# Retention's up projection in seven-product units, after the pooling branch's

## The chip, the cores and the metric

The kernel runs on one core of a Trainium2 chip. The metric is the device time of one execution in microseconds (us). The kernel before has a median of 1364.72 us over 3 runs (1364.48 to 1365.15).

## The reference: one decoder block with two token mixers

Input x is 1024 tokens by 1024 features in float32. One layer computes

```
h  = rmsnorm(x);  z = h @ w_in          # q | k | v | g | pool channels | gate logits
ret_n = group_norm(retention(q, k, v))  # 4 heads, chunks of 128 tokens
y_ret  = (silu(g) * ret_n * gn_gain) @ w_ret_up            # 1024 -> 1024
p[g]   = mean over the last 2/4/8/16 tokens of pool channels - the token itself
y_pool = (group_linear(p) * pool_scale) @ w_pool_up        # 512 -> 1024
gates  = sigmoid(gate_logits + b_gate)                     # 2 x 1024
x  = x + (gates_A * y_ret + gates_B * y_pool) @ w_o
x  = x + relu(rmsnorm(x) @ w_up)^2 @ w_down                # 4096 wide
out = rmsnorm(x)
```

## The kernel before

Activations are kept feature-major: 8 tiles (f = 0 to 7) of 128 features by 1024 tokens, in two halves of 512 tokens. Every float32 operand of a matmul is a *pair*: its rounding to fp32r (an ACTIVATE Copy on ScalarE) and the remainder (a subtraction on VectorE); `split_pair` (L133) makes one for 128x512. A product of two pairs takes three matmul passes, `PASSES` (L114).

A plain projection (`feature_major`, L126) multiplies 8 k-tiles by 3 passes for each output tile and half: 24 matmuls of 128x512. The other form is the *unit*: `Unit` (L180) and `seven` (L212) treat weight and activation as 2 x 2 blocks and form the four output blocks of two feature tiles, over both token halves, from seven block products (B11, T2, B21, T1, T3, B22, T4) instead of eight. A block product is 4 k-tiles by 3 passes, 12 matmuls; a unit has 84. For this a unit makes four sums of weight blocks (L202) and seven weight pairs, one `pair_tile` of tag "a" each (L203), and seven sets of four activation pairs (`hx` or `h2`) must exist. The results meet in PSUM banks X, Y, Z and V: p1 is a copy of X, u2 = p1 - Y, u4 = u2 + Z, and `done(m, half, ps, add)` takes each finished block on. With `late=True` (the first unit of a row) k = 3 comes after k = 0 to 2 of all four banks.

The order of the work:

1. q, k, v and retention per head (L480 to L494). `transposed` (L468) writes the normalized result to retn_dram.
2. `pool_input` (L502) makes the pooling channels and stores them in u_dram; `mixed_blocks` (L512) makes the activation sums T1 to T4 as `hx`.
3. Twelve mixer units (`mixer_unit`, L541). Units 0 to 3 are swish units: they make g, its swish from a Sigmoid and a product (L566 to L570), multiply it with ret_n and store the result in ret_dram. Units 4 to 11 are gate units: Sigmoid (L573), stored in sg_dram, tiles 0 to 7 for retention (A) and 8 to 15 for pooling (B). In unit 11, `load_ret` (L584) reads ret_dram back as 16 pairs retT.
4. Retention's up projection as a plain one (L630 to L641, ps_yr): 8 tiles, each multiplied by its gate from sg_dram (L638). After every second tile comes one group of pooling (`pool`, L604): VectorE's window sums and `exact` products with pool_w (ps_pw), giving ypT.
5. Pooling's up projection (L643 to L660, ps_yp), its gate, the sum with retention's part, and the pairs mixT.
6. The output projection (L698 to L723, ps_o), plain, which also makes x1, its squares and `h2`.
7. Sixteen up units (`up`, L732) and the down projection (L860 on).

Three things set the order. The kernel is written in program order, and the Tile framework's scheduler places each instruction on its engine's queue when, by its own timing, operands and buffers are there, earlier instructions first; on the chip each queue then runs in that fixed order. Buffers come from pools by tag: "h" and "r" have 16 tiles each and "a" 9 (L68), 4 KB per partition each; `wpool` has 4 weight tiles, `rpool` 2 "raw" tiles; PSUM has 5 "mm" and 3 "aux" banks. An instruction that needs a tile waits until an old one of its tag is let go. And loads go through SyncE's queue (SP), stores and some loads through GpSimd's (POOL).

Of the kernel before, what the change touches and what calls it, by code (L numbers as in the profile page):

```python
# [10 lines left out]
F32 = mybir.dt.float32  # L11
# [5 lines left out]
P = 128  # L17
# [5 lines left out]
NH = 4  # L23
# [15 lines left out]
def block_kernel(ctx: ExitStack, tc: tile.TileContext, a: dict, out: bass.AP):  # L39
# [12 lines left out]
    idle = apool.tile([P, HALF], mybir.dt.bfloat16, tag="a", name="idle", bufs=9)  # L52
# [13 lines left out]
    mask = consts.tile([P, NH, CH], F32, name="mask")  # L66
    corr = consts.tile([P, 4, 16], F32, name="corr")
    BUFS = {"h": 16, "r": 16, "a": 9}  # L68
# [47 lines left out]
    def product(ps, nk, stationary, moving):  # L116
        n = nk * len(PASSES)
        i = 0
        for k in range(nk):
            for sa, sb in PASSES:  # L120
                nc.tensor.matmul(  # L121
                    ps, stationary(k, sa), moving(k, sb), start=i == 0, stop=i == n - 1
                )
                i += 1

    def feature_major(ps, w, x, half, nk=KT, j0=0):  # L126
        product(
            ps, nk,
            lambda k, s: w[:, s, k, j0 : j0 + P],
            lambda k, s: x[k][half][:, s, :],  # L130
        )
# [48 lines left out]
    class Unit:  # L180


        def __init__(self, name, src):
            self.name, self.ws = name, {}
# [12 lines left out]

        def stationary(self, x):
            if x not in self.ws:
                src, *adds = self.made[x]  # L200
                for dst, u, v in adds:
                    nc.vector.tensor_tensor(dst, u, v, ALU.add)  # L202
                self.ws[x] = pair_tile("a", f"w{x}_{self.name}")  # L203
                split_pair(self.ws[x], src)
            return self.ws[x]
# [80 lines left out]
    R1 = a_tile("a", "R1")  # L286
# [181 lines left out]
    def transposed(h, rn):  # L468
        for e in range(2):
            dst = a_tile("a", f"retn{h}_{e}")  # L470
# [31 lines left out]
    def pool_input(g):  # L502
        w = load_piece(a["w_fm"][8 + g], f"w_pu{g}")
        u = a_tile("a", f"u{g}")
        for half in range(2):
            sl = slice(half * HALF, (half + 1) * HALF)
            ps = mm_bank(f"ps_pu{g}_{half}")
            feature_major(ps, w, hT, half)
            nc.scalar.activation(u[:, sl], ps, AF.Copy)
        nc.gpsimd.dma_start(u_dram[g], u)  # L510
# [27 lines left out]
    ret_dram = dram_tile("ret_dram", (KT // 2, P, 2, S))  # L538
    sg_dram = dram_tile("sg_dram", (2 * KT, P, S))

    def mixer_unit(i, first=None, after=None):  # L541
# [9 lines left out]
        def done(m, half, ps, add=None):  # L551
# [3 lines left out]
            if swish:  # L555
                t = rpool.tile([P, 2, HALF], F32, tag="raw", name=f"sw{f}_{half}")
                z, sig = t[:, 0, :], t[:, 1, :]
            else:
                z = ps if add is None else dst
# [4 lines left out]
            if swish:  # L564
                nc.vector.scalar_tensor_tensor(z, y, sign, R1[:, sl], ALU.mult, ALU.mult)
                nc.scalar.activation(sig, z, AF.Sigmoid)  # L566
                nc.vector.scalar_tensor_tensor(
                    dst, dst, vec[:, V_GNG + f : V_GNG + f + 1], sig, ALU.mult, ALU.mult
                )
                nc.vector.tensor_tensor(dst, dst, z, ALU.mult)  # L570
            else:
                nc.vector.tensor_tensor(z, y, R1[:, sl], ALU.mult)
                nc.scalar.activation(  # L573
                    dst, z, AF.Sigmoid, scale=sign, bias=vec[:, V_BG + f : V_BG + f + 1]
                )
            left[m] -= 1
            if not left[m]:
                nc.gpsimd.dma_start(ret_dram[f // 2, :, f % 2, :] if swish else sg_dram[f], o[m])
# [3 lines left out]
    retT = []  # L582

    def load_ret():  # L584
        for p2 in range(KT // 2):
            r2 = w_tile(f"ret{p2}", F32).rearrange("p (i t) -> p i t", i=2)
            nc.sync.dma_start(r2, ret_dram[p2])
            for i in range(2):
                retT.append([])
                for half in range(2):  # L590
                    dst = pair_tile("h" if p2 < 2 else "r", f"retT{2 * p2 + i}_{half}")
                    split_pair(dst, r2[:, i, half * HALF : (half + 1) * HALF])
                    retT[-1].append(dst)

    for i in range(12):
        mixer_unit(i, first_mx if i == 0 else None, load_ret if i == 11 else None)


    pw_raw, pw = a_tile("r", "pw_raw", shape=(P, HALF)), pair_tile("r", "pw")
    nc.sync.dma_start(pw_raw, a["pool_w"])  # L600
    split_pair(pw, pw_raw)
    ypT = []

    def pool(g):  # L604
        win = WINDOWS[g]
        u = a_tile("r", f"uf{g}")
        nc.sync.dma_start(u, u_dram[g])
        nc.vector.tensor_tensor(u, u, R1, ALU.mult)
        cur = u
        step = 1  # L610
        while step < win:
            nx = a_tile("r", f"s{g}_{step}")
# [6 lines left out]
        ypT.append([])  # L619
        for half in range(2):  # L620
            pooled = pair_tile("r", f"pooled{g}_{half}")
            split_pair(pooled, cur[:, half * HALF : (half + 1) * HALF])
            ps = aux_bank(f"ps_pw{g}_{half}")
            exact(ps, lambda s: pw[:, s, g * P : (g + 1) * P], lambda s: pooled[:, s, :])
            dst = pair_tile("h", f"ypT{g}_{half}")
            split_scaled(dst, ps, vec[:, V_PSC + g : V_PSC + g + 1])
            ypT[g].append(dst)

    mixed = []
    for f in range(KT):  # L630
        w = load_piece(a["w_ret"][f], f"w_ret{f}")
        m = a_tile("a", f"m{f}")
        nc.sync.dma_start(m, sg_dram[f])
        for half in range(2):
            sl = slice(half * HALF, (half + 1) * HALF)
            ps = mm_bank(f"ps_yr{f}_{half}")
            feature_major(ps, w, retT, half)
            nc.vector.tensor_tensor(m[:, sl], m[:, sl], ps, ALU.mult)  # L638
        mixed.append(m)
        if f % 2:  # L640
            pool(f // 2)  # L641
    mixT = []
    for f in range(KT):  # L643
        if f % 2 == 0:
            w = load_piece(a["w_pool"][f // 2], f"w_po{f}", cols=256)
            sg = w_tile(f"sgb{f}", F32).rearrange("p (i t) -> p i t", i=2)
            nc.sync.dma_start(sg, sg_dram[KT + f : KT + f + 2].rearrange("i p t -> p i t"))
        m = mixed[f]
        pairs = []
        for half in range(2):  # L650
# [3 lines left out]
            y = sg[:, f % 2, sl]  # L654
            nc.vector.tensor_tensor(y, y, ps, ALU.mult)
            nc.vector.tensor_tensor(m[:, sl], m[:, sl], y, ALU.add)
            dst = pair_tile("h", f"mixT{f}_{half}")
            split_pair(dst, m[:, sl])
            pairs.append(dst)
        mixT.append(pairs)  # L660
# [36 lines left out]

    for k in range(4):  # L698
# [4 lines left out]
        ws = {}  # L703
        for n, (f, half) in enumerate(order):
            if k == 3 and n == 1:
                first_up = Unit("up0", a["w_up"][0]).begin(B11, T2, T1, T3)
            if f not in ws:
                x1[f] = a_tile("a", f"x1_{f}")
                nc.gpsimd.dma_start(x1[f], a["xT"][f * P : (f + 1) * P, :])
                ws[f] = load_piece(a["w_o"][f], f"w_o{f}")  # L710
                gained[f] = a_tile("r", f"gained{f}")
            sl = slice(half * HALF, (half + 1) * HALF)
            ps = mm_bank(f"ps_o{f}_{half}")
            feature_major(ps, ws[f], mixT, half)
# [8 lines left out]
        moving_operands(h2, k, gained[k], gained[k + 4], "r" if k < 2 else "h")  # L723
# [8 lines left out]
    def up(j):  # L732
# [8 lines left out]
        def done(m, half, ps, add=None):  # L741
# [16 lines left out]
            Unit(f"up{j}", a["w_up"][j]) if j else first_up, h2, done, late=j == 0,  # L758
# [137 lines left out]
    u4s = [a_tile("a", f"u4_{i}", shape=(P, 2, HALF)) for i in range(2)]  # L896
# [195 lines left out]
```

## Time and profile before

| | before |
|---|---|
| median of 3 runs | 1364.72 us |
| the profiled execution | 1365.59 us, its span 1363.5 us |
| mixer units, from unit 0's second pass to the end of unit 11 | 297.9 to 512.6 us |
| ps_yr with ps_pw | 512.6 to 605.9 us |
| ps_yp | 605.9 to 649.4 us |
| ps_o | 649.4 to 740 us, some up products among it |
| VectorE busy in ps_yp's stretch | 32.79 of 43.5 us |

The profile is one execution on the chip. PE is TensorE, PEld its weight loads, DVE VectorE, ACT ScalarE, POOL GpSimd, SP SyncE. L12 is line 12 of the kernel. A group of instructions is shown as `out<-in`, partitions x elements, count, busy time, mean ns of one, and the idle time of the engine before it with what ended it. The chain is the work that ended last, followed back from the end; its rows give start, length and what ran. A wait's row gives the total, the number of times and the longest. A DMA's row ends with the size and the median time from issue to landing.

### The profile page before, as it was taken

To read this page: it belongs to the slowest core of one execution; us is meant where nothing else is said; L and a number is where in the kernel's file an instruction comes from. 1 tells how busy PE (TensorE), PEld (TensorE's weight loads), DVE (VectorE), ACT (ScalarE), POOL (GpSimd) and SP (SyncE) were. 2 spreads that over 40 slices of the span, in tenths; PEclk is the share of its full clock that TensorE was granted. 3 is DMA by queue.
4 is the path that set the end of the run, shared out by engine and by line. 5 is a ranking of instruction groups with operands and counts; after the bars stand their busy time and mean duration, and the time that the engine had idled before them with its cause. 6 is when DMAs were issued, how large, how long until landed. Compare 5 with 4: busy or idle time off the path is not lost.

```text
span 1363.5 us, 17493 instructions
## 1 busy us (share of the span) xinstructions
PE 1350.9 (99%) x6572; PEld 1137.6 (83%) x6572; DVE 988.8 (73%) x1627; ACT 569.0 (42%) x968; POOL 85.6 (6%) x151
## 2 busy tenths in 40 slices
PE   9999999999999999999999999999999999999997
PEld 6998989888888888888888888888888888888886
DVE  5765565689966668728667888877787967689675
ACT  6224425564334343113445443343433544444372
POOL 0000001111000000000000011110111000000000
PEclk9999999999999999999999999999999999999999
DMA  9112021364352266224422244433438989778423
GB/s 361 50 63 77 17 93 63 100 240 170 108 185 90 97 249 236 77 78 170 139 93 81 112 170 170 170 127 128 170 140 311 410 315 360 257 267 310 152 71 124
DMA packets 65444, 225.07 MB, mean 165 GB/s; under 512 B 7376, under 2 KB 9424, under 8 KB 61264
## 3 DMA queue, kind: packets, MB, share of 16 engines
q1 hardware_dynamic: 47152, 158.66, 32.9%
q0 software_dynamic: 17920, 65.02, 12.6%
q8 instruction: 51, 0.84, 0.2%
q10 hardware_dynamic: 288, 0.29, 0.1%
q14 instruction: 33, 0.27, 0.1%
HBM read 167.31 MB, written 56.62 MB: 164 GB/s over the span
## 4 chain that ended last, share of the span: by engine, by line
PE 93%; DMA 2%; issue 2%; ACT 1%; DVE 1%; POOL 0%; SPq 0%; POOLq 0%; DVEq 0%; ACTq 0%
PE ps_v L121 7%; PE ps_o L121 6%; PE ps_yr L121 6%; PE ps_dnZ L864 6%; PE ps_Xup L219 6%; PE ps_dnX L864 6%; PE ps_Zup L219 6%; PE ps_dnV L864 6%; PE ps_Vup L219 6%; PE ps_Xmx L219 5%; PE ps_Zmx L219 4%; PE ps_Vmx L219 4%; PE ps_kT L121 3%; PE ps_yp L121 3%; PE ps_pu L121 3%; PE ps_qT L121 3%
## 5 line engine op out<-in xcount | busy, mean ns | idle before, releaser
L121 PE MATMUL ps_v<-w_v_hi,hT 128*128 128x256 f32 x512 | 96.0, 284 | 0.0
L134 ACT ACTIVATE w_up<-raw_up 128x512 fp32r<-128x512 f32 x96 | 58.5, 627 | 89.6 <-DVE raw_up L202 45.4
L219 PE MATMUL ps_Xup<-mv,w_up 128*128 128x512 f32 x384 | 93.2, 390 | 0.0
L864 PE MATMUL ps_dnX<-db,da 128*128 128x512 f32 x384 | 93.0, 389 | 0.1
L219 PE MATMUL ps_Zup<-mv,w_up 128*128 128x512 f32 x384 | 92.8, 389 | 0.0
L219 PE MATMUL ps_Vup<-mv,w_up 128*128 128x512 f32 x384 | 92.4, 389 | 0.0
L121 PE MATMUL ps_yr<-retT,w_ret 128*128 128x512 f32 x384 | 88.3, 389 | 0.5 <-ACT w_ret L94 0.5
L121 PE MATMUL ps_o<-mixT,w_o 128*128 128x512 f32 x384 | 87.7, 389 | 0.0
L121 PEld LDWEIGHTS ps_yr<-retT,w_ret 128*128 128x128 f32 x384 | 72.0, 188 | 15.8 <-ACT w_ret L94 0.9
L864 PEld LDWEIGHTS ps_dnX<-db,da 128*128 128x128 f32 x384 | 72.0, 188 | 15.4 <-DVE db L135 0.5
L219 PEld LDWEIGHTS ps_Vup<-mv,w_up 128*128 128x128 f32 x384 | 72.1, 188 | 15.0
L219 PEld LDWEIGHTS ps_Zup<-mv,w_up 128*128 128x128 f32 x384 | 72.1, 188 | 14.9
L121 PEld LDWEIGHTS ps_o<-mixT,w_o 128*128 128x128 f32 x384 | 72.0, 188 | 15.0
L219 PEld LDWEIGHTS ps_Xup<-mv,w_up 128*128 128x128 f32 x384 | 71.9, 188 | 14.9
L135 DVE TENSOR_TENSOR w_up<-raw_up,w_up 128x512 fp32r<-128x512 f32 x96 | 64.6, 687 | 26.2 <-ACT w_up L134 26.1
L121 PEld LDWEIGHTS ps_v<-w_v_hi,hT 128*128 128x128 f32 x512 | 80.7, 192 | 0.0
L134 ACT ACTIVATE w_mx<-raw_mx 128x512 fp32r<-128x512 f32 x72 | 43.7, 628 | 81.4 <-DVE raw_mx L202 39.7
L121 PE MATMUL ps_v<-w_v_lo,hT 128*128 128x256 f32 x256 | 72.6, 284 | 0.0
L219 PE MATMUL ps_Xmx<-hT,w_mx 128*128 128x512 f32 x288 | 69.8, 389 | 0.0
L219 PE MATMUL ps_Vmx<-hx,w_mx 128*128 128x512 f32 x288 | 69.5, 389 | 0.0
L739 ACT ACTIVATE act<-act 128x512 f32<-128x512 f32 x64 | 40.2, 629 | 62.7 <-DVE act L738 60.6
L219 PEld LDWEIGHTS ps_Vmx<-hx,w_mx 128*128 128x128 f32 x288 | 54.1, 188 | 11.2
(250 smaller groups left out, 2826.3 us busy)
## 6 DMA issues: line engine op xcount, KB each, us to landing
act_dram<-act POOLq DMA_DIRECT2D x48, 512.0 KB, 4.3
ad<-act_dram SPq DMA_DIRECT2D x48, 512.0 KB, 6.4
raw_up<-in_w_up_dram SPq DMA_DIRECT2D x16, 1024.0 KB, 4.9
raw_mx<-in_w_mix_dram SPq DMA_DIRECT2D x12, 1024.0 KB, 6.0
sg_dram<-mx POOLq DMA_DIRECT2D x16, 512.0 KB, 4.7
wa_lo<-in_w_down_dram SPq DMA_DIRECT2D x16, 512.0 KB, 9.0
wb_hi<-in_w_down_dram SPq DMA_DIRECT2D x16, 512.0 KB, 7.1
wc_lo<-in_w_down_dram SPq DMA_DIRECT2D x16, 512.0 KB, 5.2
```

The lines of the kernel that those rows point to most:

```text
L121: nc.tensor.matmul(ps, stationary(k, sa), moving(k, sb), start=i == 0, stop=i == n - 1)
L134: nc.scalar.activation(dst[:, 0, :], src, AF.Copy)
L135: nc.vector.tensor_tensor(dst[:, 1, :], src, dst[:, 0, :].bitcast(F32), ALU.subtract)
L219: nc.tensor.matmul(ps, w[:, sa, k * P : (k + 1) * P], moving[x][k][:, sb, :], start=start and k == 0 and n == 0, stop=k == 3 and n == 2, s ...
L739: nc.scalar.activation(dst, dst, AF.Square)
L864: nc.tensor.matmul(banks[i][:, c0 : c0 + n], w[:, sa, i * P : (i + 1) * P], x[:, sb, c0 : c0 + n], start=start and j == 0 and m == 0, stop ...
```

## The change

Retention's up projection becomes four units `ret_unit(i)` with output tiles i and i + 4, and it now comes after pooling's up projection.

- *Operand sums.* A swish unit, when both its tiles are finished, makes from them the sums T1, T3, T2 and T4 on VectorE and stores them in rt_dram. Swish itself is one Silu; the product after it is gone.
- *Pooling* moves from between the tiles of ps_yr to behind gate units 4, 6, 7 and 8. Its result goes to yp_dram and comes back in unit 11 as the pairs ypT.
- *ps_yp* multiplies gate B, loaded into `mixed[f]`, in place. During it `ret_operands` loads and splits the sets `rx`: B11 ahead of f = 0, T2 at f = 2, T1 and T3 at f = 4, B21 with B22 and T4 behind the loop (`RET_AT`). The weight pair of the first retention unit is begun at f = 6.
- *The retention units* load gate A (sga, two "raw" tiles; unit 3 a weight tile), multiply and add into `mixed`, and make mixT as soon as a tile is finished.
- *The output projection*, for k = 0, first runs the k-tiles of `early` in four banks, and k-tiles 3 and 7 afterwards. Both weights of a k are loaded at its start.
- *Buffers.* "a" goes from 9 to 5; a new tag "e" of 4 takes R1, retn, u, the window sums, rt, yf, m4 to m7 and x1. `rx` stands in "r" (B11, T2, T1, T3) and "h" (B21, B22, T4), mixT in "r" instead of "h", and `h2` the other way round. The up units take their weight pairs from "a" and "e" in turn.

The diff, cut to its core:

```diff
-    BUFS = {"h": 16, "r": 16, "a": 9}
+    BUFS = {"h": 16, "r": 16, "a": 5, "e": 4}
...
+                tag = self.tags[len(self.ws) % len(self.tags)]
+                self.ws[x] = pair_tile(tag, f"w{x}_{self.name}")
                 split_pair(self.ws[x], src)
...
-                nc.scalar.activation(sig, z, AF.Sigmoid)
+                nc.scalar.activation(z, z, AF.Silu)
                 nc.vector.scalar_tensor_tensor(
-                    dst, dst, vec[:, V_GNG + f : V_GNG + f + 1], sig, ALU.mult, ALU.mult
+                    dst, dst, vec[:, V_GNG + f : V_GNG + f + 1], z, ALU.mult, ALU.mult
                 )
-                nc.vector.tensor_tensor(dst, dst, z, ALU.mult)
...
+            if swish and not any(left):
+                l0, l1, h0, h1 = token_blocks(*o)
+                t = [a_tile("e", f"rt{i}_{j}", shape=(P, 2, HALF)) for j in range(2)]
+                t1, t3, t2, t4 = t[0][:, 0, :], t[0][:, 1, :], t[1][:, 0, :], t[1][:, 1, :]
+                for dst, x, y, op in (
+                    (t1, l0, l1, ALU.subtract), (t3, h1, l1, ALU.subtract),
+                    (t2, h1, t1, ALU.add), (t4, t2, h0, ALU.subtract),
+                ):
+                    nc.vector.tensor_tensor(dst, x, y, op)
+                for j in range(2):
+                    nc.gpsimd.dma_start(rt_dram[i, j], t[j])
...
+        two = [a_tile("e", f"win{g}_{i}") for i in range(min(2, win // 2))]
...
+        nc.gpsimd.dma_start(yp_dram[g], y)
...
+    RET_AT = {0: (B11,), 2: (T2,), 4: (T1,), 8: (B21, T4)}
...
+    def pooled_operands():
+        for g in range(4):
+            y = a_tile("e", f"yf{g}")
+            nc.sync.dma_start(y, yp_dram[g])
+            ypT.append([pair_tile("h", f"ypT{g}_{half}") for half in range(2)])
+            for half in range(2):
+                split_pair(ypT[g][half], y[:, half * HALF : (half + 1) * HALF])
...
+    def ret_operands(*steps):
+        def pair(x, k, src):
+            rx[x][k] = pair_tile("h" if x in (B21, B22, T4) else "r", f"rx{x}_{k}")
+            split_pair(rx[x][k], src)
...
+        for step in steps:
+            if step in (T2, T4, B11):
+                for k in (0, 2):
+                    raw = block(*(
+                        ret_dram[k + i][:, :HALF] if step == B11
+                        else rt_dram[k + i, 1, :, int(step == T4), :] for i in range(2)
+                    ))
+                    for i in range(2):
+                        pair(step, k + i, raw[:, i, :])
+            else:
+                for k in range(4):
+                    if step == T1:
+                        raw = block(rt_dram[k, 0, :, 0, :], rt_dram[k, 0, :, 1, :])
+                    else:
+                        raw = block(ret_dram[k + 4][:, :HALF], ret_dram[k + 4][:, HALF:])
+                    pair(step, k, raw[:, 0, :])
+                    pair({T1: T3, B21: B22}[step], k, raw[:, 1, :])
...
+    BESIDE = dict(zip((4, 6, 7, 8), range(4)))
+    for i in range(12):
+        mixer_unit(i, first_mx if i == 0 else None, pooled_operands if i == 11 else None)
+        if i in BESIDE:
+            pool(BESIDE[i])
...
+        if f in RET_AT:
+            ret_operands(*RET_AT[f])
+        m = mixed[f] = a_tile("h" if f < 4 else "e", f"m{f}")
+        nc.sync.dma_start(m, sg_dram[KT + f])
...
+            first_ret = Unit("ret0", a["w_ret"][0]).begin(B11)
+    ret_operands(*RET_AT[8])
...
+    def ret_unit(i, first=None):
+        tiles = (i, i + 4)
+        unit = first or Unit(f"ret{i}", a["w_ret"][i])
+        if i < 3:
+            gates = [rpool.tile([P, S], F32, tag="raw", name=f"sga{f}") for f in tiles]
+        else:
+            nc.gpsimd.memset(unit.u4[:, :1], 0.0)
+            gates = w_tile("sga3", F32).rearrange("p (i t) -> p i t", i=2)
+            gates = [gates[:, m, :] for m in range(2)]
+        for m, f in enumerate(tiles):
+            nc.sync.dma_start(gates[m], sg_dram[f])
+        if i == 3:
+            for f in (0, 4):
+                w_o[f] = load_piece(a["w_o"][f], f"w_o{f}")
+        left = [2, 2]
+        def done(m, half, ps, add=None):
+            sl = slice(half * HALF, (half + 1) * HALF)
+            dst, gate, y = mixed[tiles[m]][:, sl], gates[m][:, sl], ps
+            if add is not None:
+                y = {(1, 1): unit.p1, (0, 1): unit.u4, (1, 0): unit.u2}[m, half]
+                nc.vector.tensor_tensor(y, add, ps, ALU.add)
+            nc.vector.scalar_tensor_tensor(
+                gate, y, -1.0 if m else 1.0, gate, ALU.mult, ALU.mult
+            )
+            nc.vector.tensor_tensor(dst, dst, gate, ALU.add)
+            left[m] -= 1
+            if not left[m]:
+                f = tiles[m]
+                mixT[f] = [pair_tile("r", f"mixT{f}_{h}") for h in range(2)]
+                for h in range(2):
+                    split_pair(mixT[f][h], mixed[f][:, h * HALF : (h + 1) * HALF])
+        seven(unit, rx, done, late=bool(first))
+    for i in range(4):
+        ret_unit(i, first_ret if i == 0 else None)
...
+    early = (0, 4, 1, 5, 2, 6)
...
+        for f in (k, k + 4):
+            ws[f] = w_o.pop(f, None) or load_piece(a["w_o"][f], f"w_o{f}")
+            if k == 0:
+                for half in range(2):
+                    banks[f, half] = mm_bank(f"ps_o{f}_{half}")
+                    feature_major(banks[f, half], ws[f], mixT, half, ks=early)
...
+            if k == 0:
+                ps = banks[f, half]
+                feature_major(ps, ws[f], mixT, half, ks=(3, 7))
+            else:
+                ps = mm_bank(f"ps_o{f}_{half}")
+                feature_major(ps, ws[f], mixT, half)
...
```

More of the change, by code (lines that the diff above doesn't have):

```diff
@@ L51, in block_kernel @@
     nc.scalar.preload_act_table_set("sigmoid_and_others")
-    idle = apool.tile([P, HALF], mybir.dt.bfloat16, tag="a", name="idle", bufs=9)
+    idle = apool.tile([P, HALF], mybir.dt.bfloat16, tag="a", name="idle", bufs=5)
     nc.vector.memset(idle, 0.0)
@@ L114, in block_kernel, with product, feature_major @@
     PASSES = ((0, 0), (0, 1), (1, 0))
[L116 to L120, printed above, removed]
+    def product(ps, nk, stationary, moving, ks=None):
+        for k in ks or range(nk):
+            for i, (sa, sb) in enumerate(PASSES):
                 nc.tensor.matmul(
-                    ps, stationary(k, sa), moving(k, sb), start=i == 0, stop=i == n - 1
-                )
-                i += 1
-    def feature_major(ps, w, x, half, nk=KT, j0=0):
+                    ps, stationary(k, sa), moving(k, sb),
+                    start=k == 0 and i == 0, stop=k == nk - 1 and i == len(PASSES) - 1,
+                )
+    def feature_major(ps, w, x, half, nk=KT, j0=0, ks=None):
         product(
@@ L130, in feature_major @@
             lambda k, s: x[k][half][:, s, :],
+            ks,
         )
@@ L555, in done @@
             if swish:
-                t = rpool.tile([P, 2, HALF], F32, tag="raw", name=f"sw{f}_{half}")
-                z, sig = t[:, 0, :], t[:, 1, :]
+                t = rpool.tile([P, HALF], F32, tag="raw", name=f"sw{f}_{half}")
+                z = t
             else:
@@ L595, in block_kernel @@
[L595 to L602, printed above, removed]
+                nc.gpsimd.dma_start(ret_dram[f] if swish else sg_dram[f], o[m])
+            if swish and not any(left):
[9 more added lines that the diff above has]
+                    nc.gpsimd.dma_start(rt_dram[i, j], t[j])
@@ L618, in pool @@
         nc.vector.scalar_tensor_tensor(cur, cur, 1.0 / win, u, ALU.mult, ALU.subtract)
[L619 to L633, printed above, removed]
+        pw = consts.tile([P, 2, P], F32R, tag="mask", name=f"pw{g}")
+        pw_raw = rpool.tile([P, P], F32, tag="raw", name=f"pw_raw{g}")
+        nc.sync.dma_start(pw_raw, a["pool_w"][:, g * P : (g + 1) * P])
+        split_pair(pw, pw_raw)
+        y = rpool.tile([P, S], F32, tag="raw", name=f"yp{g}")
         for half in range(2):
@@ L635, in block_kernel @@
             sl = slice(half * HALF, (half + 1) * HALF)
[L636 to L642, printed above, removed]
-    for f in range(KT):
[L644 to L649, printed above, removed]
+            pooled = pair_tile("e", f"pooled{g}_{half}")
@@ new lines, in pool @@
+            split_pair(pooled, cur[:, sl])
+            ps = aux_bank(f"ps_pw{g}_{half}")
+            exact(ps, lambda s: pw[:, s, :], lambda s: pooled[:, s, :])
+            nc.scalar.activation(
+                y[:, sl], ps, AF.Copy, scale=vec[:, V_PSC + g : V_PSC + g + 1]
+            )
+        nc.gpsimd.dma_start(yp_dram[g], y)
+    RET_AT = {0: (B11,), 2: (T2,), 4: (T1,), 8: (B21, T4)}
+    ypT = []
+    mixed = [None] * KT
+    def pooled_operands():
[5 more added lines that the diff above has]
+                split_pair(ypT[g][half], y[:, half * HALF : (half + 1) * HALF])
@@ new lines, in block_kernel, with block @@
+    rx = [[None] * 4 for _ in range(7)]
+    def ret_operands(*steps):
+        def pair(x, k, src):
+            rx[x][k] = pair_tile("h" if x in (B21, B22, T4) else "r", f"rx{x}_{k}")
+            split_pair(rx[x][k], src)
+        def block(*srcs):
+            raw = rpool.tile([P, 2, HALF], F32, tag="raw", name="rb")
+            for i, src in enumerate(srcs):
+                nc.sync.dma_start(raw[:, i, :], src)
+            return raw
+        for step in steps:
[15 more added lines that the diff above has]
+                    pair({T1: T3, B21: B22}[step], k, raw[:, 1, :])
@@ L757, in up @@
         seven(
-            Unit(f"up{j}", a["w_up"][j]) if j else first_up, h2, done, late=j == 0,
+            Unit(f"up{j}", a["w_up"][j], "ae") if j else first_up, h2, done, late=j == 0,
             opened=None if j else token_scales, after=begin_down if j == NJ - 1 else None,
```

70 lines of the change are left out of this document (28 added, 42 removed).

## The prediction

> **What bounds the kernel now.** I read the page first: span, busy shares, clock, the chain that ended last.
>
> ```profile
> span 1363.5 us, 17493 instructions
> PE 1350.9 (99%) x6572; PEld 1137.6 (83%) x6572; DVE 988.8 (73%) x1627; ACT 569.0 (42%) x968; POOL 85.6 (6%) x151
> PEclk9999999999999999999999999999999999999999
> PE 93%; DMA 2%; issue 2%; ACT 1%; DVE 1%; POOL 0%; SPq 0%; POOLq 0%; DVEq 0%; ACTq 0%
> ```
>
> TensorE is busy for 99% of the span at full granted clock and holds 93% of the chain. A pipelined matmul counts as busy longer than it holds the engine, so I looked next at who TensorE waited for, and at how fast the chain's long pieces run.
>
> ```profile
> PE ps_yr L121 <- ACT w_ret L94: 0.5, 1, 0.5
> PE ps_dnV L864 <- ACT dt L134: 0.5, 1, 0.5
> ...
> 311.45 2.72 PE ps_Zmx L219 x12
> ...
> 582.91 21.76 PE ps_yr L121 x96
> 606.03 43.52 PE ps_yp L121 x192
> ```
>
> In the stage that changes, the waits of TensorE come to one, of 0.5 us, on the first weight of retention's up projection. The chain's pieces give the true price of a 128x512 product: 21.76/96 = 43.52/192 = 2.72/12 = 0.2267 us. This is the same in a seven-product unit (L219) and in a plain product (L121). The path from the mixer units to the end of the output projection is a row of matmuls at this pitch, so time is won by issuing fewer, provided their operands are there in time.
>
> **The change part by part: the matmuls removed.**
>
> ```profile
> L121 PE MATMUL ps_yr<-retT,w_ret 128*128 128x512 f32 x384 | 88.3, 389 | 0.5 <-ACT w_ret L94 0.5
> L371 PE MATMUL ps_pw<-pooled,pw 128*128 128x512 f32 x24 | 6.4, 389 | 0.0
> ```
>
> Before: 8 feature tiles x 2 halves x 8 k-tiles x 3 passes = 384. After: 4 units x 7 products x 4 k-tiles x 3 passes = 336. The 24 pooling matmuls move but stay, as do the 192 of ps_yp and 384 of ps_o. Saved: 48 x 0.2267 = **10.88 us**. The 0.5 us wait of ps_yr goes too (pooling's up projection is now the stage that follows the units; what it may wait for is counted below).
>
> **VectorE in the stages.** Busy counts overlap, so I took the issue pitch from its timeline.
>
> ```profile
> 350.21 1.89 DVE L135 TENSOR_TENSOR w_mx<-raw_mx,w_mx 128x512 fp32r<-128x512 f32 x3
> ...
> 559.56 1.23 DVE L95 TENSOR_TENSOR w_ret<-raw_w_ret,w_ret 128x1024 fp32r<-128x1024 f32 x1 [0.40 <-ACT w_ret L94]
> 560.70 1.22 DVE L608 TENSOR_TENSOR uf<-uf,R 128x1024 f32<-128x1024 f32 x1
> ...
> L135 DVE TENSOR_TENSOR w_mx<-raw_mx,w_mx 128x512 fp32r<-128x512 f32 x72 | 48.3, 688 | 7.0 <-ACT w_mx L134 6.6
> L567 DVE SCALAR_TENSOR_TENSOR mx<-mx,vec,sw 128x512 f32<-128x512 f32 x16 | 12.0, 749 | 0.0
> L570 DVE TENSOR_TENSOR mx<-mx,sw 128x512 f32<-128x512 f32 x16 | 10.9, 690 | 0.1
> ```
>
> One 512-wide operation lasts 0.69 us, but three take 1.89, so the pitch is (1.89 - 0.69)/2 = 0.60 us; a 1024-wide one has 560.70 - 559.56 = 1.14. TensorE needs 7 x 2.72 = 19.04 us per unit.
>
> ```profile
> 316.70:335.80 19.10, 19.10 (x86) 15.80 (x85) 17.54 (x29) 7.27 (x12) 2.40 (x5) 1.00 0.45 166
> 392.90:412.00 19.10, 19.10 (x86) 15.83 (x85) 11.57 (x19) 7.45 (x12) 1.06 (x2) 1.00 0.34 110
> 605.90:649.40 43.50, 43.50 (x194) 36.03 (x193) 32.79 (x49) 13.93 (x20) 2.47 (x5) 1.00 0.46 161
> ```
>
> These are one swish unit, one gate unit and the whole of ps_yp: length, then busy time of PE, PEld, DVE, ACT, POOL.
>
> *Swish units (0 to 3).* A unit has 4 weight sums, 7 splits, u2, u4 and 3 additions, so 16, and 12 swish operations: 28. The change drops the last product (L570, 4 per unit) and adds 4 operand sums: 28 again, 28 x 0.60 = 16.8 us plus 0.06 for each L567 = 17.0 of 19.04. The row shows 17.5 and TensorE at no loss: cost 0, covered by 2 us of spare time. On POOL's queue rt_dram's two stores per unit, which wait for the sums, now stand ahead of the next unit's loads from retn_dram. These come at most 4 x 0.60 = 2.4 us later, wanted first by done(0,0) 8 us into the unit; without that cover three units would pay up to 2.4.
>
> *Before the units* u and retn move to tag "e": 4 slots, R1 holds one.
>
> ```profile
> 266.51 0.57 POOL L510 DMA_DIRECT2D u_dram<-u  x1 [2.03 <-ACT u L509]
> ...
> 283.63 0.54 POOL L510 DMA_DIRECT2D u_dram<-u  x1 [3.12 <-ACT u L509]
> u_dram<-u POOLq DMA_DIRECT2D x4, 512.0 KB, 7.4
> ```
>
> u0's slot is free at 266.5 + 7.4 = 273.9; u3, complete at 283.6, wants it for its first half some 24 x 0.2267 = 5.4 us earlier, at 278. Cost 0 by 4 us; a later store would hold up ScalarE and with it the first weights.
>
> *Gate units (4 to 11)* have 16 + 4 = 20 operations, 12.0 us. Pooling comes beside units 4, 6, 7 and 8 with 3, 4, 5 and 6 wide operations and about 1.9 us of splits and slivers each: 18 x 1.14 + 4 x 1.9 = 28 us. Over units 4 to 8 VectorE has 60 + 28 = 88 us against 5 x 19.04 + 24 x 0.2267 = 100.6 on TensorE. Only unit 8 alone is over (12 + 6 x 1.14 + 1.9 = 20.7 against 20.4), and unit 9 has 7 us free. Cost 0. The second half of ypT's split (8 scalar_tensor_tensor) becomes plain splits in unit 11, where retT's 16 stood.
>
> *ps_yp* now carries 16 gate multiplications, some 22 operand splits, 8 operations for the first weights and 2 to 4 wide ones: 46 x 0.60 + 3 x 1.14 = 31 us of 43.5. It fits.
>
> *Retention units.* 16 + 8 = 24 operations (14.4 us) in units 0 to 2, since mixT has no slots then: tag "r" has 16, and B11, T2, T1 and T3 hold all of them until unit 3 has used them. Unit 3 gets 24 + 16 mixT splits + 2 wide ones = 40 x 0.60 + 2.28 = 26.3 us against 19.04. The surplus of 7.2 is hidden by ps_o's early part, 4 x 18 matmuls = 16.3 us that need neither mixT 3 nor 7. Without that cover it would cost 7.
>
> **Waits that the change may add.** None is in the trace of before, so each has two ends.
>
> ```profile
> L51 ACT ACT_TABLE_LOAD x1 | 1.3, 1283 | 0.7 <-PEq L1082 0.7
> L566 ACT ACTIVATE sw<-sw 128x512 f32<-128x512 f32 x16 | 10.0, 628 | 10.4 <-DVE sw L565 10.4
> ```
>
> *Silu* replaces Sigmoid in the swish units and Sigmoid returns in the gates. If that means two table loads, they take 2 x 1.283 = 2.57 us of ScalarE, which is busy 7.3 of 19.1 us in a swish unit. Behind the load on its queue stand the weight splits, and the first falls in unit 0, where weights are least ahead. Ends 0 and 2.6; I take **0.5**, near the idle share. The Trainium skill (ScalarE: Activation LUTs, What ACT_TABLE_LOAD costs) prices a switch to another set at about 2.66 us with its drain, and asks that calls be batched by set; by it the upper end would be an estimated 5.3. The load alone agrees with this trace's 1283 ns; no run here shows a drain.
>
> *Fewer weight slots.* Tag "a" goes from 9 (R1 holds one) to 5.
>
> ```profile
> 311.38 1.30 DVE L135 TENSOR_TENSOR w_mx<-raw_mx,w_mx 128x512 fp32r<-128x512 f32 x2
> ...
> 319.61 1.81 PE ps_Ymx L219 x8
> ```
>
> The pair for T2 is written at 311.4 and first used at 319.6: 8 us ahead. Five slots still allow 4 products ahead, 10.88 us. But at unit 0 two are held by head 3's rn until its transposes end, so T3's pair is later. Ends 0 and 1.32 per unit (one split on ScalarE, 0.63, and VectorE, 0.69, exposed); I take **0.6** once, at unit 0.
>
> *Units to ps_yp.* Eight pairs of ypT wait for hT's slots, as retT's did: 0 to 2, taken **0.5**, what the entry cost before.
>
> *ps_yp to retention unit 0.*
>
> ```profile
> ret_dram<-mx POOLq DMA_DIRECT2D x8, 512.0 KB, 4.3
> m<-sg_dram SPq DMA_DIRECT2D x8, 512.0 KB, 6.6
> raw_w_o<-in_w_o_dram SPq DMA_DIRECT2D x8, 512.0 KB, 4.0
> wa_lo<-in_w_down_dram SPq DMA_DIRECT2D x16, 512.0 KB, 9.0
> ```
>
> All operand blocks and the gates go through two "raw" buffers, in turn. B21/B22 of k = 2, 3 find "h" slots when ypT goes, so their splits end some 0.3 us after ps_yp; then T4's two blocks load (4 us), are split (2), and only then the two gates load (4), landing at about 10. The gate is wanted when X is complete: 36 + 3 + 3 + 12 matmuls, 54 x 0.2267 = 12.2 us after the start. It is 2 us in time with loads of 4.0; with loads of 9.0 it lands at 20 and VectorE stands before u4, for which B22 on Z waits at 13.6: about 8 us. Ends 0 and 8; I take **1.0**, nearest the 4.0 of a quiet queue. On SP the waiting gate load holds back the next unit's weights, which have 10 us to spare.
>
> *The rest* (the gates of units 1 to 3, the up units' weights in turn in "a" and "e", w_o's loads one k earlier, x1's loads on POOL behind the memset, and 2 MB each way of yp_dram while DMA is at 0.34 in a gate unit and 0.46 in ps_yp): 0 to 3, taken **0.6**.
>
> **The sum.** -10.88 - 0.5 + 0.5 + 0.6 + 0.5 + 1.0 + 0.6 = -8.2. The profiled run took 1365.59 us (2.1 around its span), so 1357.4; the median of the runs is 0.87 lower, hence 1364.72 - 8.2 = **1356.5**.
>
> **The rivals.**
> *All covered*: every added wait is hidden, -11.4, 1353.3. For it: TensorE waits only about 0.5 us anywhere in this stretch now. Against: new boundaries that share two raw buffers.
> *Tables exposed*: the loads fall on the path, 2.6 instead of 0.5: 1358.6. For: little work ahead in unit 0. Against: ScalarE idles over half of each unit. It rests on the rule of ScalarE: Activation LUTs in the Trainium skill about sets.
> *Late gates*: loads at 9.0 us, unit 0 stalls 8 instead of 1: 1363.5. For: 14 blocks, 8 gates and 4 weights load in ps_yp. Against: DMA has been busy at most half in these stages.
> *Slower: the look-ahead is too short.* The place is each seven-product unit in "a" alone (12 mixer, 4 retention); T2's pair waits behind three sums and the previous unit's results. If the three products by which 8 slots shrink to 5 (8.2 us) are taken out of the 8 us seen, one split of 1.32 us is exposed per unit: 16 x 1.32 = 21.1, and 1364.72 - 11.4 + 21.1 = 1374.4. It turns the result once the mean wait exceeds 11.4/16 = 0.71 us per unit. Against it: lead is also bounded by VectorE's order, and 10.88 us of slots remain.
> *The change doesn't do what it says*: the order by priority could run the pooling elsewhere than beside the gates; it has 100.6 - 88 us spare there, so this costs at most the 1.4 us of one pair of ps_pw products that waits.
>
> **How the numbers follow.** Forecast 0.58, all covered 0.12, tables exposed 0.08, late gates 0.11, look-ahead 0.08, pooling elsewhere 0.03. A measurement here tells about 0.2% (2.7 us) from no change, so faster means below 1362.0. The first three and the last are faster (0.81), and so is a share of 0.02 of the late gates: 0.83. The rest of those gives 0.07 same and 0.02 slower, with look-ahead 0.10 slower. The range runs from 1352.9 (all covered, with 0.4 for spread) to 1363.5 (late gates), which leaves out the slower cases and the worst of the late gates.
>
> **What would show it.** ps_Xret, Yret, Zret and Vret total 336 matmuls with pieces of 2.72 us in the chain; the waits of TensorE list no weight pair above 1 us; two more ACT_TABLE_LOAD rows; DVE at about 15 of 19 us in retention units 0 to 2 and full in unit 3; gates (sga) landing before X is complete. I am wrong if TensorE's waits name w_mx, w_ret or sga with more than 5 us in all, or if a unit's period exceeds 19.04 throughout.

## The result and the profile after

The changed kernel has a median of 1352.53 us (1351.91 to 1353.48, 5 runs), beside 1365.15 us for the kernel before in the same comparison. The ratio is 0.9909, 95% interval [0.9894, 0.9923]. So it is faster by 12.6 us, where 8.2 were forecast, and lies 0.4 us below the low end of the range. The profiled execution took 1351.91 us, 13.68 less than that of before; its span is 13.4 shorter.

First the page: span, busy time and chain.

```profile
span 1350.1 us, 17637 instructions
PE 1338.8 (99%) x6524; PEld 1128.7 (84%) x6524; DVE 1024.1 (76%) x1698; ACT 593.7 (44%) x1017; POOL 92.2 (7%) x164
PE 97%; DVE 1%; issue 1%; DMA 0%; ACT 0%; SPq 0%; POOLq 0%; POOL 0%; DVEq 0%; ACTq 0%
```

TensorE has the 48 matmuls less (6572 to 6524) and now holds 97% of the chain instead of 93%. VectorE does 35 us more work, all of it beside matmuls. The chain's pieces give the pitch:

```profile
524.36 36.15 PE ps_yp L119 x159
...
574.57 2.72 PE ps_Zret L219 x12
578.42 2.72 PE ps_Vret L219 x12
```

A product costs what it cost before (36.15/159 = 2.72/12 = 0.227 us), also in retention's units. The next view is the whole list of TensorE's waits:

```profile
PE awake L56 <- DVE idle L53: 1.2, 1, 1.2
PE ps_qT L119 <- DVE hT L138: 1.1, 3, 0.5
PE spread_z L155 <- POOL rstd_z L149: 1.1, 1, 1.1
PE ps_dnV L947 <- ACT dt L133: 0.5, 1, 0.5
PE sums_z L165 <- ACT sq_z L1066: 0.5, 1, 0.5
PE ps_qT L119 <- ACT hT L137: 0.3, 1, 0.3
```

All of them lie at the start of the kernel or from the down projection's last block on. None is in the changed stretch: neither w_mx, w_ret, sga nor ps_yp is named. But two waits of before are gone, and the prediction had counted only the one at ps_yr. The other stood in the same list, directly above the ps_yr row that the prediction shows, and in the timeline of before, where retention's last head ends:

```profile
PE ps_pu L121 <- ACT u L509: 0.7, 1, 0.7
```

```profile
264.17 1.06 ACT L447 ACTIVATE rn<-ps_ret 128x512 f32<-128x512 f32 x2
...
264.56 0.52 PE L371 MATMUL ps_ret<-sp,qp 128*128 128x256 f32 x3
265.12 2.55 ACT L509 ACTIVATE u<-ps_pu 128x512 f32<-128x512 f32 x5
265.77 2.58 PE L121 MATMUL ps_pu<-hT,w_pu 128*128 128x512 f32 x10 [0.69 <-ACT u L509]
```

ScalarE copies five halves of u in a row, and only right behind head 3's rn (the brackets hold the idle time before a row and what ended it). The products that fill those banks had been done earlier; there are five "mm" banks, all were full, and TensorE stood still. Both u and rn were tiles of tag "a". In the changed kernel u is of tag "e", its first copy is at 233.65, and TensorE goes through:

```profile
266.51 0.52 PE L371 MATMUL ps_ret<-sp,qp 128*128 128x256 f32 x3
266.87 3.36 PE L119 MATMUL ps_pu<-hT,w_pu 128*128 128x512 f32 x14
```

To see where the 13.4 us went I took, for each matmul of both traces, the time to the start of the next, less 0.2267:

| | us |
|---|---|
| 48 matmuls fewer | -10.9 |
| ps_pu, behind head 3 (0.85) and in its products (0.12) | -1.0 |
| entry from the mixer units to the next projection, 0.8 to 0.1 | -0.7 |
| ps_o and the up unit's products among it, 0.83 to 0.23 | -0.6 |
| first products of q, which vary from trace to trace | -0.3 |
| waits added | 0 |
| sum (the spans differ by 13.4) | -13.5 |

The changed kernel, run again beside the last experiments, gave 1352.90 us (1352.60 to 1353.25, 4 runs), ratio 0.9911 [0.9897, 0.9924]. Its median lies on the low end of the range, not below it. In its trace a wait does show, at the first retention unit: 0.7 us in the list, 0.95 by the counting of the table; more on that under the last experiments.

### The profile page after: what moved, and what is told of

Read it like the earlier page. It is cut to its first block, busy times and chain, and to the rows that moved or that the text cites. A ratio compares the mean times of both kernels' runs of the same rounds, so it can differ in the third digit from the quotient of the medians.

```text
span 1350.1 us, 17637 instructions
## 1 busy us (share of the span) xinstructions
PE 1338.8 (99%) x6524; PEld 1128.7 (84%) x6524; DVE 1024.1 (76%) x1698; ACT 593.7 (44%) x1017; POOL 92.2 (7%) x164
## 4 chain that ended last, share of the span: by engine, by line
PE 97%; DVE 1%; issue 1%; DMA 0%; ACT 0%; SPq 0%; POOLq 0%; POOL 0%; DVEq 0%; ACTq 0%
PE ps_v L119 7%; PE ps_o L119 6%; PE ps_Xup L219 6%; PE ps_Zup L219 6%; PE ps_Vup L219 6%; PE ps_dnX L947 6%; PE ps_dnZ L947 6%; PE ps_dnV L947 6%; PE ps_Xmx L219 5%; PE ps_Zmx L219 5%; PE ps_Vmx L219 5%; PE ps_pu L119 3%; PE ps_Yup L219 3%; PE ps_yp L119 3%; PE ps_kT L119 3%; PE ps_qT L119 3%
## 5 line engine op out<-in xcount | busy, mean ns | idle before, releaser
L219 PEld LDWEIGHTS ps_Xmx<-hT,w_mx 128*128 128x128 f32 x288 | 54.0, 188 | 11.2
L134 DVE TENSOR_TENSOR w_mx<-raw_mx,w_mx 128x512 fp32r<-128x512 f32 x72 | 48.7, 688 | 4.2 <-ACT w_mx L133 3.8
```

The lines of the kernel that those rows point to most:

```text
L134: nc.vector.tensor_tensor(dst[:, 1, :], src, dst[:, 0, :].bitcast(F32), ALU.subtract)
L219: nc.tensor.matmul(ps, w[:, sa, k * P : (k + 1) * P], moving[x][k][:, sb, :], start=start and k == 0 and n == 0, stop=k == 3 and n == 2, s ...
```

## The experiments

The theory: the row of matmuls is the whole of the price, one product for one product; the waits that I priced at +3.2 together are hidden, and waits of before that I had not priced at all have gone. The rivals: the look-ahead in tag "a" is at its limit (one more slot costs 1.3 us a unit); the cover in ps_o and the place of the pooling are worth many microseconds; the missing product of the swish, not the shape of the stages, is what was gained.

**One product more in each retention unit.**

```diff
+        if name.startswith("ret"):
+            mult(X, B11)
```

> Each retention unit issues B11's product twice (the first result is overwritten): 48 matmuls of 128x512 more than after, no other work. If the path is a row of matmuls at 0.2267 us and the waits that I had priced at 3.2 us are not there: 1352.5 + 48 x 0.2267 = 1363.4 us, TensorE's pitch unchanged. If those waits are there and only outweighed by gains elsewhere, the 2.7 us more per unit hide part of them: 1360.2 to 1362.9.

Measured: 1363.19 us (11 runs, 1361.67 to 1365.66), ratio 0.9986 [0.9977, 0.9995]. That is 10.7 above the changed kernel, for 48 x 0.2267 = 10.9. The biggest term of the sum is right in kind and size.

**One product less.**

```diff
-        mult(V, T4, start=False)
+        if name.startswith("ret"):
+            unit.stationary(T4)
+        else:
+            mult(V, T4, start=False)
```

> Each retention unit leaves out the 12 matmuls of T4's product (so one of its four output blocks lacks that product); T4's operands are still loaded and split. A unit is then 16.3 us on TensorE and VectorE has 24 x 0.60 = 14.4 us in it. Row of matmuls with cover to spare: 1352.5 - 10.9 = 1341.6 us. Waits near the surface (the gates of unit 0, VectorE in unit 3): 1343 to 1347, with sga, mixT or w_ret among TensorE's waits.

Measured: 1343.69 us (1343.38 to 1344.85, 4 runs), ratio 0.9844 [0.9831, 0.9857]: 8.8 less, not 10.9. The number lies where waits near the surface were expected, but none of the three names given for them (sga, mixT, w_ret) is in TensorE's list. These are, and they make up most of the other 2 us:

```profile
PE ps_yp L119 <- DVE mx L566: 0.7, 1, 0.7
PE ps_o L119 <- ACT w_o L94: 0.6, 1, 0.6
...
PE ps_Zret L219 <- DVE tmp_ret L244: 0.2, 1, 0.2
```

The wait at ps_yp lies ahead of the retention units and comes and goes in the other kernels too (see the last experiments). The other two are at the last retention unit: when the four units are 2.7 us shorter each, w_o and the unit's results come late. By the counting of the table the last unit and ps_o lose 1.7 us more here than in the changed kernel. So there is cover behind the last unit, and four products less use it up.

**The output projection without the early k-tiles.**

```diff
-            if k == 0:
-                for half in range(2):
-                    banks[f, half] = mm_bank(f"ps_o{f}_{half}")
-                    feature_major(banks[f, half], ws[f], mixT, half, ks=early)
...
-            if k == 0:
-                ps = banks[f, half]
-                feature_major(ps, ws[f], mixT, half, ks=(3, 7))
-            else:
-                ps = mm_bank(f"ps_o{f}_{half}")
-                feature_major(ps, ws[f], mixT, half)
+            ps = mm_bank(f"ps_o{f}_{half}")
+            feature_major(ps, ws[f], mixT, half)
```

> The output projection of k = 0 in plain order, k-tiles 0 to 7 for each tile and half; all else as in after. By the prediction's price for this cover, VectorE's surplus of 7.2 us in unit 3 comes out: 1359.5 us. If the order of TensorE's queue fills such a gap by itself with k-tiles 0 to 2 of the four banks (4 x 9 x 0.2267 = 8.2 us): 1352.5 to 1353.5.

Measured: 1353.26 us (1352.59 to 1353.89, 4 runs), ratio 0.9912 [0.9899, 0.9926]: no difference from the changed kernel that can be told. No wait in ps_o is in its list at all; it has 0.7 us at ps_yp and 1.1 at ps_Xret, both ahead of what the edit touches. So the 7 us that the prediction hid behind this early part don't come out when the early part is left out.

**Two of the five slots of "a" taken away.**

```diff
+    held = [a_tile("a", f"held{i}") for i in range(2)]
+    for t in held:
+        nc.vector.memset(t[:, :1], 0.0)
...
+    for t in held:
+        nc.vector.tensor_copy(t[:, :1], mixed[7][:, :1])
```

> From mixer unit 0 to the end of the last retention unit two of tag a's five tiles are held by unused tiles, so weight pairs have 3 slots and can be 2 products (5.4 us) ahead. The rival of the look-ahead (one split of 1.32 us exposed per unit as soon as the lead is short): 16 x 1.32 = 21 more, 1374 us. Cover to spare: 1352.5 to 1353.5.

Measured: 1353.13 us (1352.65 to 1356.13, 5 runs), ratio 0.9922 [0.9908, 0.9936]. In the trace, whose run took 1352.65, one wait of the kind is new, once in all sixteen units:

```profile
PE ps_Vret L219 <- ACT w_ret L133: 0.5, 1, 0.5
```

The rival of the look-ahead falls: it gave 21 us, and three slots do nearly as well as five. Two of the five runs, not profiled, took about 1356; what they wait for is not known. The 8 us by which a pair was ahead were no need.

**u back in the slots of "a", and out of them in the kernel before.** Two kernels, each with one line changed: the changed kernel with `u = a_tile("a", f"u{g}")`, the kernel before with `u = a_tile("r", f"u{g}")`.

> The kernel after with u in tag a instead of e. If the shared tag is the cause, ScalarE copies u only after rn of head 3, TensorE waits 0.7 to 0.9 us for u again, and the time is 1353.4 us; if not, 1352.5.

Measured: 1354.56 us (1354.11 to 1357.06, 5 runs), ratio 0.9928 [0.9915, 0.994], 1.7 to 2.0 above the two medians of the changed kernel.

```profile
PE ps_yp L119 <- DVE mx L563: 1.7, 1, 1.7
...
PE ps_pu L119 <- ACT u L509: 0.7, 1, 0.7
```

The wait on u is back with the size that it had before, 0.7 (0.97 by the counting of the table), so the tag is its cause. The entry to ps_yp takes another 1.9 in this trace; more on it below. Whether u's tag has a part in that is not shown.

> The kernel before with the pooling channels u in tag r instead of a. If TensorE's 0.85 us gap in the pooling channels' stage comes from u's tiles standing behind head 3's rn in tag a (u's first copy runs right after rn's second tile is first written), then u is copied out earlier, that wait is gone and the time is 1364.3 us; if u's copies are late for another reason, the gap stays and so does 1365.15.

Measured: 1368.07 us (11 runs, 1366.73 to 1368.82), ratio 1.0022 [1.0013, 1.0031]: slower, though the wait on u is gone from its list. Another has grown:

```profile
PE ps_yr L121 <- ACT w_ret L94: 2.8, 1, 2.8
```

It was 0.5 in the kernel before. In the timeline ScalarE's queue holds four splits of retT ahead of the first weight of ps_yr, and they had waited for ret_dram's loads:

```profile
511.00 2.19 ACT L134 ACTIVATE retT<-ret 128x512 fp32r<-128x512 f32 x4 [0.72 <-DMA ret<-ret_dram]
513.10 0.71 ACT L573 ACTIVATE mx<-mx,vec 128x512 f32<-128x512 f32 x1
513.71 1.99 ACT L94 ACTIVATE w_ret<-raw_w_ret 128x1024 fp32r<-128x1024 f32 x2
514.80 1.65 PE L121 MATMUL ps_yr<-retT,w_ret 128*128 128x512 f32 x3 [2.83 <-ACT w_ret L94]
```

The granted clock falls behind this stop, to 0.66 from 514 to 519 us, and with the products slowed by it the entry costs 3.8 us more than before; less the 1.0 of u, that is about the 3 us by which this kernel is slower. So u's new tag is worth 1 us in the changed kernel, and in the kernel before this one line gains nothing. Why the first weight comes 2.3 us later here is not settled.

**Sigmoid and the product instead of Silu.**

```diff
...
-                nc.scalar.activation(z, z, AF.Silu)
+                nc.scalar.activation(sig, z, AF.Sigmoid)
...
-                    dst, dst, vec[:, V_GNG + f : V_GNG + f + 1], z, ALU.mult, ALU.mult
+                    dst, dst, vec[:, V_GNG + f : V_GNG + f + 1], sig, ALU.mult, ALU.mult
                 )
+                nc.vector.tensor_tensor(dst, dst, z, ALU.mult)
```

> The kernel after with the swish of before: Sigmoid and a product on VectorE instead of Silu, so no table loads behind the first one and 32 VectorE operations per swish unit (4 more). If the two table loads cost what I took, 0.5 us, and the products are covered: 1352.0 us. VectorE then has 32 x 0.60 + 0.24 = 19.4 us for 19.04 in each of four units; if that comes out, 1.6 more, 1354.1. If both are hidden: 1352.5.

Measured: 1355.15 us (1351.78 to 1356.43, 5 runs), ratio 0.9924 [0.9911, 0.9936]. The median is above all three forecasts. Its best run is as fast as the best of the changed kernel; its profiled one is 4.2 slower than the profiled one there, and nearly all of that lies in one place, long after the swish units:

```profile
524.40 3.56 PE L119 MATMUL ps_yp<-ypT,w_po 128*128 128x512 f32 x15
528.09 2.65 ACT L133 ACTIVATE rx<-rb 128x512 fp32r<-128x512 f32 x4 [5.48 <-DMA rb<-rt_dram]
528.76 0.69 DVE L134 TENSOR_TENSOR rx<-rb,rx 128x512 fp32r<-128x512 f32 x1 [6.97 <-ACT rx L133]
529.37 0.68 DVE L563 TENSOR_TENSOR mx<-tmp_mx,ps_Vmx 128x512 f32<-128x512 f32 x1
...
530.10 5.08 PE L119 MATMUL ps_yp<-ypT,w_po 128*128 128x512 f32 x14 [2.14 <-DVE mx L563]
```

Read it from the top: the load of T2's block lands late; ScalarE's split has waited 5.48 us for it, VectorE's split 6.97 for ScalarE; the next instruction on VectorE's queue evicts the last mixer unit's V bank; and that bank is what ps_yp's next products need. The fourteen products behind it take 5.08 us instead of 14 x 0.2267 + 0.16 = 3.33 (0.16 is the end of the last one, 0.389 - 0.227), so the wait costs 2.14 + 1.75 = 3.9. Without it the run would stand at an estimated 1352.3. The swish itself can't be told apart: neither this trace nor that of the changed kernel has a wait of TensorE in the swish units, so VectorE's four operations a unit and the two table loads are both covered.

**Pooling beside the swish units instead of the gates.**

```diff
-    BESIDE = dict(zip((4, 6, 7, 8), range(4)))
+    BESIDE = dict(zip(range(4), range(4)))
```

> Pooling beside swish units 0 to 3 instead of gate units 4, 6, 7 and 8. By the prediction's count VectorE has 4 x 17.0 + 28 = 96 us there against 4 x 19.04 + 5.4 = 81.6 on TensorE, 14.5 over. With weight pairs at most 10.9 us ahead at least 3.6 of it comes out, at most all: 1356 to 1367 us, with w_mx or pooled among TensorE's waits. If late results can be put off without holding TensorE: 1352.5 to 1354.

Measured: 1397.09 us (1394.88 to 1399.96, 5 runs), ratio 1.0237 [1.0223, 1.0251]: 44.6 more than the changed kernel, about three times the highest expectation. First the waits, then the stretches (length, then busy time of PE, PEld, DVE, ACT, POOL, the granted clock, DMA's share and GB/s):

```profile
PE ps_Zmx L219 <- DVE w_mx L134: 7.1, 2, 5.1
PE ps_Xmx L219 <- ACT w_mx L133: 6.1, 4, 1.9
PE ps_Xmx L219 <- DVE w_mx L134: 5.0, 4, 1.4
```

```profile
320.00:345.00 25.00, 21.78 (x86) 17.07 (x86) 16.78 (x26) 7.38 (x12) 2.14 (x4) 0.90 0.33 113
...
370.00:400.00 30.00, 19.45 (x63) 13.62 (x61) 18.49 (x30) 9.44 (x15) 2.67 (x5) 0.83 0.35 125
```

Weight pairs are late, but VectorE is busy only 16.78 of 25 and 18.49 of 30 us, and 101.7 of 133.5 in all five stretches from 296.5 to 430 us: short of time in places, it also waits in its own order. TensorE's longest wait shows one such place, first on VectorE, then on TensorE:

```profile
382.31 0.17 DVE L605 COPY win<-win 128x2 f32<-128x2 f32 x1 [3.08 <-DMA rt_dram<-rt]
...
383.52 0.68 DVE L134 TENSOR_TENSOR w_mx<-raw_mx,w_mx 128x512 fp32r<-128x512 f32 x1
...
384.25 4.63 PE L219 MATMUL ps_Zmx<-hx,w_mx 128*128 128x512 f32 x10 [5.09 <-DVE w_mx L134]
```

A window sum waits 3.08 us until a store of the operand sums rt has let go a slot of "e", and the weight pair that TensorE needs stands behind it. How much of the 44.6 comes from the shared slots no run separates. The granted clock is lower too: 0.97, 0.90, 0.93, 0.83 and 0.83 in the five stretches. What is missing to 1, times their lengths, is 0.7 + 2.5 + 1.8 + 5.1 + 5.1 = 15 us; at most so much of the 44.6 is the clock, since TensorE also stood idle in part of that time.

**The first T2 splits later, and earlier.** These two test the cause read from the sigmoid kernel: a split that waits for its load, one place ahead of an eviction. The changed kernel has `RET_AT = {0: (B11,), 2: (T2,), 4: (T1,), 8: (B21, T4)}`; the first has `{0: (B11,), 3: (T2,), 5: (T1,), 8: (B21, T4)}`, the second `{0: (B11, T2), 4: (T1,), 8: (B21, T4)}`. They ran beside the changed kernel itself.

> T2 (operand of retention's unit products, read back from rt_dram) is loaded and split from the second half of k = 3 of ps_yp on, not from k = 2 on, so that on VectorE no split that waits for a load stands ahead of the last eviction (L563) of the last mixer unit's Vmx bank, which ps_yp's first products wait for; T1 moves from k = 4 to k = 5. My theory: this queue place is what varies from run to run at the entry to ps_yp (0.1 us over nominal in the first profile of the changed kernel, 1.0, 2.0 and 4.1 us in three variants): here ps_yp stands within 0.3 us of nominal, the median is 1351.5 to 1352.3, and no run is above 1353.5. Rival (the loads themselves are slow at this boundary and whatever needs them waits, T2's user instead): the runs spread as before, up to 1355 or 1356, the median is 1352.5 to 1353.5, and the wait shows at ps_Xret or further on in ps_yp.

Measured: 1354.04 us (1353.66 to 1355.68, 5 runs), ratio 0.9922 [0.9908, 0.9935]. At the entry to ps_yp it does what the theory says:

```profile
523.93 6.28 PE L119 MATMUL ps_yp<-ypT,w_po 128*128 128x512 f32 x27
524.13 0.69 DVE L563 TENSOR_TENSOR mx<-tmp_mx,ps_Vmx 128x512 f32<-128x512 f32 x1 [3.14 <-PE ps_Vmx L219]
527.98 2.65 ACT L133 ACTIVATE rx<-rb 128x512 fp32r<-128x512 f32 x4 [6.17 <-DMA rb<-rt_dram]
...
571.30 1.38 ACT L133 ACTIVATE rx<-rb 128x512 fp32r<-128x512 f32 x2 [2.38 <-DMA rb<-rt_dram]
572.59 0.58 ACT L236 ACTIVATE tmp_ret<-ps_Xret 128x512 f32<-128x512 f32 x1
...
573.22 3.06 PE L219 MATMUL ps_Xret<-rx,w_ret 128*128 128x512 f32 x12 [2.15 <-ACT tmp_ret L236]
```

The load is as late as in the sigmoid kernel (ScalarE waits 6.17 us for it), but the eviction is ahead of it at 524.13 and TensorE doesn't notice. As to the total, the rival is right, and its wait is at ps_Xret: the stream of loads ends late, its last split starts at 571.30 us, and behind it on ScalarE's queue stands the copy of X, which the first retention unit waits 2.2 us for. That order is the changed kernel's too, where the same split starts at 567.62 and 570.02 us in its two traces. All five runs here are above all those of the changed kernel beside them, but that the edit made the last load late isn't shown: without the early k-tiles, with this part unchanged, the split starts at 571.14 us.

> T2 is prepared from k = 0 of ps_yp on: its first two loads are issued ahead of the four loads of m, and T2's first split stays ahead of the last eviction of Vmx on VectorE. My theory: the split still stands there but its load lands early enough: median 1351.5 to 1352.6, ps_yp within 0.5 us of nominal. Rival (the place on VectorE alone matters): ps_yp 1 to 4 us over nominal in some runs, median 1353 to 1355. A third way: m's first loads, now later, hold up the first results of ps_yp, and the wait names m: 1352.5 to 1354.

Measured: 1352.65 us (1352.14 to 1353.22, 4 runs), ratio 0.9909 [0.9895, 0.9923].

```profile
PE ps_yp L119 <- DVE mx L563: 1.0, 1, 1.0
```

No wait at ps_Xret, but 1.0 at ps_yp (1.3 by the counting of the table). So the median is where my theory had it, but ps_yp isn't: the load still came late for the split ahead of the eviction.

> The changed kernel again, unaltered, as the base for the two others in this call. My theory: 1351.9 to 1353.5, with a run-dependent wait of 0 to 2 us at the entry to ps_yp. Rival (the first profile was typical and the spread of the variants came from their edits): all runs within 1351.5 to 1352.8.

Measured: the 1352.90 given above. Two of the four runs are above the rival's 1352.8, so some spread is the changed kernel's own. There is no wait at ps_yp, where I expected one, but this one:

```profile
PE ps_Xret L219 <- ACT tmp_ret L236: 0.7, 1, 0.7
```

No version beats the changed kernel by more than runs of one kernel differ. The stretch between the mixer units and the first retention unit has a wait of 0 to some 2 us left at its beginning, at its end or, without the early k-tiles, at both, depending on when the loads land. The DMA engines are busy there, which I take to be why loads land late; but the share alone doesn't decide it, since the changed kernel's trace, without a wait, has 0.94 (columns as above):

```profile
518.00:526.00 8.00, 8.00 (x37) 6.62 (x36) 3.99 (x6) 2.73 (x5) 0.53 (x1) 1.00 0.94 350
```

## Why the prediction was right in direction and short in size

*The matmuls removed, -10.88*: right. The count is 48, the pitch unchanged, and the run with one product more pays 10.7.

*The waits that go, -0.5*: this is the first step that failed. The prediction read the wait on u in the list but looked for changes only between the units and ps_o. The diff moves u to another tag, and the prediction costed that move only for what it might add ("Cost 0 by 4 us"). It gained 1.0, shown by putting u back. At the entry to the next projection 0.7 went where 0.5 stood. Another 0.6 went at ps_o, where the kernel before has up products a little ahead of their weights and the changed kernel's order has not; that cause is read from the traces and was not tested. In all, -2.3 where the sum had -0.5.

*The waits that come, +3.2 in five terms*: the second step that failed, as sizes. Silu's tables 0.5: nothing measurable; the two loads are there and take ScalarE 1.28 us each, beside matmuls. Fewer weight slots 0.6: 0, and 0.5 once with two slots less. Units to ps_yp 0.5: at most 0.1 in the two traces of the changed kernel, 0.6 to 4 in some variants, so the place is right. Into retention unit 0, 1.0: 0 and 1 in the two traces of the changed kernel, but not for the reason given. The gates land in time (VectorE's first use of one waits for X, not for the gate); what comes late is a block of T4, whose split stands ahead of ScalarE's copy of X. The rest 0.6: nothing shows.

One habit of mine is behind some of this, though no run shows how much. I counted lead times as if TensorE ran the units in program order, one behind the other. The queue order mixes them: in the changed kernel 33 products of ps_yp stand ahead of the last V bank of the mixer units, as the first row below, of its chain, shows. And pieces of ps_o stand among unit 3's last products, also in the kernel without the early k-tiles, from whose timeline the other two rows are:

```profile
514.16 7.48 PE ps_yp L119 x33
...
637.89 3.11 PE L119 MATMUL ps_o<-mixT,w_o 128*128 128x512 f32 x13
640.84 2.88 PE L219 MATMUL ps_Vret<-rx,w_ret 128*128 128x512 f32 x12
```

So the 7 us behind `early` have other products to hide behind: the scheduler puts 23 of ps_o's ahead of unit 3's last block by itself.

*The stages of VectorE*: right. The forecast was 15 of 19 us in retention units 0 to 2, and a full unit 3; the rows below are units 0 and 3.

```profile
560.50:579.00 18.50, 18.50 (x84) 15.30 (x83) 14.93 (x25) 7.72 (x13) 0.00 (x0) 1.00 0.40 131
...
617.00:637.00 20.00, 20.00 (x90) 16.55 (x89) 19.43 (x31) 10.11 (x17) 1.60 (x3) 1.00 0.58 181
```

*The argument against late gates* ("DMA has been busy at most half in these stages") was wrong as an argument. It holds for the means of a unit, not for the boundary: the share is 0.94 around 520 us here, and it was 0.99 to 1.00 from 496 to 512 us in the kernel before already. The rival still didn't come true.

*The range*: its low end was "all covered", and that case held only the waits that I had decided to remove. A low end has to ask of every wait in the list whether the edit can touch it; here 1.6 us more could go at u and ps_o.

## What to carry to other kernels

When a buffer moves from one pool to another, go through the waits of the kernel before and ask for each whether the tile that it names, or a neighbour in its old pool, has moved: a tile can wait for a neighbour of its tag that it has nothing to do with, as u did for rn. A split of a loaded block on VectorE or ScalarE holds back everything behind it on that queue, so look at which eviction stands next. Here neither a later nor an earlier split took the wait away. Don't trust a cover that you count in program order, in either direction: the early k-tiles covered nothing that wasn't covered already, and pooling beside the swish units cost 44.6 us where the count gave at most 14.5. The queue order in the trace says what really stands there.

## What the runs showed of the hardware

*A table switch* takes 1.30 us, from the start of the load to the start of the first activation that needs it (298.55 - 297.25), at the first of the two switches in the changed kernel's timeline of ScalarE, where one activation ends at 297.23 and the next has its operand ready:

```profile
297.25 1.28 ACT L567 ACT_TABLE_LOAD   x1
298.55 1.22 ACT L567 ACTIVATE sw<-sw 128x512 f32<-128x512 f32 x2
```

The Trainium skill (ScalarE: Activation LUTs, What ACT_TABLE_LOAD costs) gives about 2.66 us with a drain; here the load's 1283 ns is there and the drain isn't, so the measurement decides for 1.3. At the second switch ScalarE waits for its next operand behind the load, so it doesn't tell.

*A short stop can slow TensorE afterwards.* Behind the sigmoid kernel's wait of 2.14 us, the fourteen products that take 1.75 us too long stand in a stretch with a lower clock:

```profile
530.00:535.00 5.00, 4.90 (x14) 3.88 (x15) 5.00 (x10) 1.42 (x3) 0.53 (x1) 0.66 0.57 175
```

The granted clock is 0.66 there, so the wait costs about twice what the list says. The 2.83 us of the kernel before with u in "r" have the same behind them, 0.66 from 514 to 519 us. But length alone doesn't decide: behind the 2.15 us of the kernel with T2 later the granted clock is 1.00 (573 to 578 us), as it is behind the 1.7 of the kernel with u back in "a". What decides isn't shown. The Trainium skill (TensorE: Matmul & The Clock Gate, HAM oscillation — how this bites in real kernels) warns of gaps over some 3.4 us; here 2.14 was enough once, and 2.15 wasn't another time.
